# Gate tiles of the state-space part go from the inverse stage to the key stage, and all eight query tiles fill the inverse stage

## The chip, the cores and the metric

The kernel runs on one core of a Trainium2 chip. The metric is the device time of one execution in microseconds (us), the median of several runs; a shorter time is better. The core's engines work side by side, each through its own instructions in a fixed order: TensorE (PE in the profile: matrix products, with PEld its weight loads), VectorE (DVE), ScalarE (ACT), GpSimd (POOL) and SyncE (SP, which here only issues DMAs).

## What is computed

One step of a two-layer trunk over 128 context tokens and 256 latent tokens, D_MODEL = 1024, in float32. The change lies in the mixer of layer 0, which runs state-space (SSD) heads and gated DeltaNet heads from one input projection:

```python
def ssd_delta_mixer(h, ssd_h0, dn_h0, w_in, w_out, ...):
    z, xbc, dt_raw, qkv, gate, a_raw, b_raw = jnp.split(h @ w_in, _offsets(L0_SIZES), axis=-1)
    ...
    y = rmsnorm(y.reshape(bsz, length, SSD_INNER) * jax.nn.silu(z.astype(F32)), ssd_norm_w)
    qkv = jax.nn.silu(dwconv(qkv, dn_conv_w))
    q, k, v = jnp.split(qkv, [DN_QK, 2 * DN_QK], axis=-1)
    q = l2norm(q.reshape(bsz, length, DN_HEADS, DN_KEY_DIM))
    k = l2norm(k.reshape(bsz, length, DN_HEADS, DN_KEY_DIM))
    ...
    o = rmsnorm(o_f + flip(o_b), dn_norm_w) * jax.nn.silu(gate.astype(F32))...
```

`gated_delta_scan` works in chunks of 128 tokens (three here: one of context, two of latents) and needs from the keys alone, for every chunk, head and direction, the inverse of a triangular 128 x 128 matrix (`triangular_solve`). The values and queries come in only after that. So z, gate and q are products that can be computed at any time before their use.

## The kernel before

The input projection of layer 0 is cut into 56 weight tiles `w0[n]` of 128 output features: 0 to 7 keys, 8 to 15 queries, 16 to 23 values, 24 to 31 B and C of the state-space part, 32 to 39 its x, 40 to 47 its gate z, 48 to 55 the DeltaNet gate g. `proj` (L648) makes one tile: 24 matmuls (L365 to L367) with 386 columns, because each weight is split into two float32r halves. For this `fetch` (L326) loads 512 KB into one of three `wst` buffers by a DMA on SP's queue, ACT casts two halves `whi` (L335), and DVE subtracts two halves `wlo` (L338). Weights are fetched in the order of `weights` (L1707), up to three tiles ahead.

What follows a tile depends on its kind. A **convolved tile** (key, query, value, B, C, x) goes through `conv` (L658): one ACT pass (L664), four DVE taps (L670), a silu on ACT; for keys and queries then three PE transposes (L698) and three squares with a sum on ACT (L1269). A **gate tile** (z, g) takes one silu on ACT (L1291), and a DMA on ACT's queue to DRAM; DVE has only its two splits.

`delta` (L1328) runs the stages around the change, one after the other:

1. **Key stage**: `scalars` and `decay` (L779: products on DVE and POOL, L788: matmuls, L791: exp on ACT) are woven with `tile_k`, the eight key tiles (the first two are already begun in `start`). It ends with a few small DVE operations on the sums of the keys' squares, the first of them `nk` (L1348).
2. **Inverse stage**: three `inverse` generators (chunk 0 at once, chunk 2 after 8, chunk 1 after 24 units of the plan's clock: `DI`) are woven with a fill of tiles, and between two tiles of the fill goes one step of `net.quads`, modulation products (L300) whose weights `wmod` take their turn in the same three `wst` buffers. Each inverse is a long chain, mostly on DVE: N (L817), forward substitution (L857, L859), NR (L839), then pairs of small matmuls (L892, L937, L946) with work of DVE (L910, L914, L932) and ACT between them.
3. **Apply stage**: first the eight value tiles, then `apply` (L980 to L1076), woven with a fill of tiles and of `fill_qk` (the q k products, L961).

`weave` (L218) orders the work when the program is built: it keeps a clock of planned costs (4.2 for a convolved tile, 3.9 for a gate tile), advances a chain when its planned wait is over, and issues the next piece of the fill in between. A fill that is used up leaves nothing to put between the chain's steps; a fill that is left over is issued at the end of the stage (`drain`). `mix(a, b, 1)` takes one piece of a and one of b in turn. What is shown as order below is the order that results on each engine.

Of the kernel before, what the change touches and what calls it, by code (L numbers as in the profile page):

```python
# [603 lines left out]
DS = [0, 0, 0, 0]  # L604
Q1 = 4
DG = ((1, 0),)
# [12 lines left out]
class Mix0:  # L619
# [53 lines left out]
    def convs(self, base, w, b, j, ns, rest, cost=4.2, first=()):  # L673
        old, late = None, None
        for n in ns:
            if n < len(first):
                ps = first[n]
                if late:
                    late()
            else:  # L680
                ps = self.proj(base + n, self.hh, self.hl, late)
            cv = self.conv(ps, w, j + n, b)
            late = old and rest(*old)
            old = n, cv
            yield cost
        if late:
            late()
        late = rest(*old)
        if late:
            late()  # L690
        yield cost - 3.8
# [578 lines left out]

    def fill_q(self, b, e):
        def rest(n, cv):
            self.nc.scalar.activation(out=self.qT[:, n, :], in_=cv, func=AF.Silu)
            return lambda: self.norms(self.totok(self.qT[:, n, :]), self.ssq, n)
        return self.convs(8, "dn_cw", None, 8, range(b, e), rest)

# [51 lines left out]
    def delta(self, A):  # L1328
# [4 lines left out]
        with ExitStack() as c1:  # L1333
# [5 lines left out]
            self.ssq = self.ts("ssq", [3, 8])  # L1339
            fill = self.tile_k()  # L1340
            net.help = HELP[0]
# [11 lines left out]
            for d in range(2):  # L1353
                v.tensor_mul(out=self.brk[:, d], in0=rk2, in1=self.beta[:, :, 8 * d:8 * d + 8])
            v.tensor_scalar_mul(out=self.nrb, in0=self.brk, scalar1=-1.0)
            self.qT = A("qT")
            fill = mix(chain(self.fill_silu(40, self.zd), self.fill_silu(48, self.gd), self.fill_q(0, Q1)),
                       chain(net.quads(0, range(4, 8), net.wst), net.quads(1, range(Q0), net.wst)), 1)
# [6 lines left out]
        with ExitStack() as c1:  # L1365
# [7 lines left out]
            drain(self.fill_v())  # L1373
            fill = chain(self.fill_q(Q1, 8), self.fill_qk(), self.fill_bc())
            weave([late(g, d) for g, d in zip(self.apply(S0), DA + [0] * 6)], fill, W0[2])
# [331 lines left out]
def weights(t):  # L1707
# [3 lines left out]
        for n in range(8) for k in range(0, KFF, 8)]  # L1711
    o1 = lambda n, i: (t["wo1"][n, :, 1024 * i:1024 * i + 1024], 1024)
    out1 = [o1(n, i) for i in range(2) for n in range(3)] + [o1(n, i) for n in range(3, 8) for i in range(2)]
    tok = lambda js: [(t["w1t"][j, i], 1024) for j in js for i in range(2)]
    return ([(t["w0s"], 512)] + one(t["w0"], [*range(8), *range(40, 56), *range(8, 8 + Q1), *range(16, 24), *range(8 + Q1, 16), *range(24, 40)])
            + [(t["wo0"][j, :, 1024 * i:1024 * i + 1024], 1024) for i in range(2) for j in range(8)] + ffn(0) + one(t["w1f"], range(3)) + tok([4, *range(4)]) + one(t["w1f"], range(3, 18)) + out1 + ffn(1))
# [35 lines left out]
```

## Time and profile before

| | us |
|---|---|
| median of 3 runs (1462.89 to 1468.02) | 1467.04 |
| the profiled execution | 1465.71 |
| its span, first to last instruction | 1463.9 |
| busy in the span: PE / DVE / ACT | 1375.5 / 959.9 / 795.9 |
| the stretch from the key stage's first tile to `nk` | 49.6 to 110.3 |
| from `nk` to NR of the third inverse (chunk 1) | 110.3 to 204.7 |
| from there to the last matmul of that inverse | 204.7 to 247.5 |
| value tiles | 247.5 to 285.2 |
| apply | 285.2 to 372.4 |

The profile is of one execution. Its own time is 1.8 us above its span and 1.3 us under the median. Busy times are of each engine for itself and overlap, so they say nothing of who waits for whom; that is read from the single stretches.

### The profile page before, as it was taken

What the parts mean: (1) busy time and instruction counts of PE and PEld (TensorE: products, weight loads), DVE (VectorE), ACT (ScalarE), POOL (GpSimd) and SP (SyncE); (2) the same over time, 40 slices, a digit from 0 to 9 for tenths busy, and PEclk for the clock granted to TensorE, in tenths of its full rate; (3) what the DMA queues carried; (4) which work ended last, traced back from release to release, by engine and by line L of the source; (5) the groups of instructions that cost most, each with busy time, mean ns of one, the idle gap of its engine ahead of it and who ended that gap; (6) DMA issues with size and microseconds to landing.
All of it is one profiled execution on the core that took longest, in us unless ns stands there. A gap on an engine that the chain in (4) does not pass through costs nothing.

```text
span 1463.9 us, 26132 instructions
## 1 busy us (share of the span) xinstructions
PE 1375.5 (94%) x10103; PEld 1292.9 (88%) x10103; DVE 959.9 (66%) x1880; ACT 795.9 (54%) x1775; POOL 196.0 (13%) x190
## 2 busy tenths in 40 slices
PE   4979979999998999999999999999999999999996
PEld 3759869999887789789999999898999899999996
DVE  3688977865978867576666444656658477767432
ACT  4577535677475336554455444644865475555341
POOL 0042200003254403300000012100002210000001
PEclk9999989999999999799999999999999999999998
DMA  9225545312643366445554443344234434434441
GB/s 366 83 89 151 172 141 173 111 44 79 210 159 106 118 200 219 145 135 168 167 165 140 120 123 109 125 134 157 87 97 163 144 101 131 118 128 126 119 130 57
DMA packets 59899, 201.57 MB, mean 138 GB/s; under 512 B 7072, under 2 KB 11824, under 8 KB 59776
## 3 DMA queue, kind: packets, MB, share of 16 engines
q1 hardware_dynamic: 52256, 185.38, 39.9%
q10 hardware_dynamic: 6192, 9.80, 1.9%
q0 software_dynamic: 1328, 4.73, 1.1%
q8 instruction: 79, 1.29, 0.4%
q14 instruction: 44, 0.36, 0.1%
HBM read 191.20 MB, written 8.68 MB: 137 GB/s over the span
## 4 chain that ended last, share of the span: by engine, by line
PE 76%; DVE 9%; issue 5%; ACT 5%; POOL 2%; DMA 2%; ACTq 0%; POOLq 0%; DVEq 0%
PE mm L380 18%; PE mm L365 10%; PE mm L366 10%; PE mm L367 10%; PE mm L382 9%; PE pmod L300 3%; DVE wlo L338 1%; POOL er L779 1%; ACT hh L454 1%; ACT t L454 1%; PE ps L479 1%; PE ps L1575 1%; PE mmt L1500 1%; DMA wst<-w 1%; PE mmt L1501 1%
## 5 line engine op out<-in xcount | busy, mean ns | idle before, releaser
L338 DVE TENSOR_TENSOR wlo<-wst,whi 128x512 fp32r<-128x512 f32 (+1 forms) x497 | 345.8, 701 | 213.3 <-ACT whi L335 209.4
L335 ACT CAST whi<-wst 128x512 fp32r<-128x512 f32 (+1 forms) x505 | 305.0, 614 | 311.2 <-PE mm L366 166.8
L380 PE MATMUL mm<-hh,whi 128*128 128x386 f32 x728 | 247.7, 340 | 3.0 <-DVE t L571 2.8
L382 PE MATMUL mm<-hl,whi 128*128 128x386 f32 x728 | 239.2, 339 | 7.5 <-DVE hl L456 7.3
L380 PE MATMUL mm<-hh,wlo 128*128 128x386 f32 x728 | 245.3, 337 | 0.0
L365 PE MATMUL mm<-hh,whi 128*128 128x386 f32 x552 | 195.5, 354 | 6.0 <-DVE t L670 6.0
L367 PE MATMUL mm<-hh,wlo 128*128 128x386 f32 x552 | 188.9, 343 | 1.7 <-DVE wlo L338 1.7
L366 PE MATMUL mm<-hl,whi 128*128 128x386 f32 x552 | 189.8, 344 | 0.0
L382 PEld LDWEIGHTS mm<-hl,whi 128*128 128x128 f32 x728 | 135.6, 188 | 11.1 <-DVE hl L456 11.0
L380 PEld LDWEIGHTS mm<-hh,whi 128*128 128x128 f32 x728 | 137.0, 188 | 6.7 <-ACT whi L335 3.1
L380 PEld LDWEIGHTS mm<-hh,wlo 128*128 128x128 f32 x728 | 136.9, 188 | 0.6 <-DVE wlo L338 0.3
L365 PE MATMUL mm<-gh,whi 128*128 128x386 f32 x352 | 119.5, 339 | 0.0
L366 PE MATMUL mm<-gl,whi 128*128 128x386 f32 x352 | 119.2, 339 | 0.0
L367 PE MATMUL mm<-gh,wlo 128*128 128x386 f32 x352 | 118.9, 338 | 0.0
L365 PEld LDWEIGHTS mm<-hh,whi 128*128 128x128 f32 x552 | 105.7, 191 | 12.5 <-issue 11.4
L569 DVE SCALAR_TENSOR_TENSOR t<-mm,vecs,t 128x385 f32<-128x385 f32 x88 | 54.3, 619 | 88.2 <-ACT t L568 88.2
L367 PEld LDWEIGHTS mm<-hh,wlo 128*128 128x128 f32 x552 | 105.2, 191 | 2.2 <-DVE wlo L338 2.1
L366 PEld LDWEIGHTS mm<-hl,whi 128*128 128x128 f32 x552 | 105.9, 192 | 0.2
L670 DVE SCALAR_TENSOR_TENSOR t<-mm,vecs,t 128x385 f32<-128x385 f32 (+1 forms) x152 | 92.1, 614 | 11.9 <-ACT t L664 6.4
L568 ACT ACTIVATE t<-mm,vecs 128x386 f32<-128x386 f32 x88 | 59.1, 676 | 70.4 <-PE mm L382 70.4
L500 POOL TENSOR_TENSOR sums<-sums,t 128x386 f32<-128x386 f32 x36 | 41.5, 1173 | 334.8 <-PE mm L366 218.1
L300 PE MATMUL pmod<-wmod,cond 128*32 128x128 f32 x1536 | 70.6, 296 | 12.9 <-ACT t L416 12.3
(421 smaller groups left out, 2586.9 us busy)
## 6 DMA issues: line engine op xcount, KB each, us to landing
wmod<-modw_l SPq DMA_DIRECT2D x96, 512.0 KB, 4.6
wst<-up_l SPq DMA_DIRECT2D x88, 512.0 KB, 3.5
wst<-w SPq DMA_DIRECT2D x56, 512.0 KB, 3.9
wst<-wo SPq DMA_DIRECT2D x32, 512.0 KB, 3.9
wst<-down_l SPq DMA_DIRECT2D x32, 512.0 KB, 3.5
wst<-w1f SPq DMA_DIRECT2D x18, 512.0 KB, 3.6
wst<-down_l SPq DMA_DIRECT2D x16, 384.0 KB, 3.1
wst<-w1t SPq DMA_DIRECT2D x10, 512.0 KB, 3.9
```

What stands on the lines that cost most here:

```text
L300: nc.tensor.matmul(acc[32 * c:32 * c + 32, 0:128], self.cond[:, k, :], w[:, o:o + 128], start=(k == 0), stop=(k == 7), tile_position=(0, 3 ...
L335: self.conv_hi = nc.scalar.copy(out=hi[:, 0:m], in_=st[:, o:o + m])
L338: self.conv_lo = eng.tensor_sub(out=lo[:, 0:m], in0=st[:, o:o + m], in1=hi[:, 0:m].bitcast(F32))
L365: mm(ps, wh, xh, start=start, stop=False)
L366: mm(ps, wh, xl, start=False, stop=False)
L367: return mm(ps, wl, xh, start=False, stop=stop)
L380: mm(ps, w[k // 4][p][:, s], hh[:, k, :], start=(k == 0 and p == 0), stop=False)
L382: mm(ps, w[k // 4][0][:, s], hl[:, k, :], start=False, stop=(k == 7))
L500: (nc.gpsimd if i else v).tensor_add(out=acc[:, i, :], in0=acc[:, i, :], in1=p)
L568: nc.scalar.activation(out=cv, in_=ps, func=AF.Identity, scale=cw(1), bias=self.v(f"ffb_l{l}", n))
L569: stt(out=cv[:, 1:T], in0=ps[:, 0:T - 1], scalar=cw(0), in1=cv[:, 1:T], op0=ALU.mult, op1=ALU.add)
L670: nc.vector.scalar_tensor_tensor(out=o, in0=p, scalar=cw(i), in1=o, op0=ALU.mult, op1=ALU.add)
```

## The change

The eight z tiles move from the fill of the inverse stage into the key stage, one behind each key tile (`mix(self.tile_k(), self.fill_silu(40, self.zd), 1)`). The fill of the inverse stage is then the eight g tiles and all eight query tiles (before: eight z, eight g, four queries), and that of the apply stage loses the other four query tiles. The list in `weights` follows, and `convs` gives the two tiles that `start` has computed a planned cost of 0. No operation is added or taken away but loads of ACT's function tables (`ACT_TABLE_LOAD`), since exp and silu now take turns more often: from the key stage up to the first g or z tile of the inverse stage 15 stand on ACT where there were 7.

```diff
--- before.py
+++ after.py
@@ -602,7 +602,7 @@
 DI = [0, 24, 8]
 DA = [0, 0, 0]
 DS = [0, 0, 0, 0]
-Q1 = 4
+NF = 2
 DG = ((1, 0),)
 MB = [8, 4]
 W1 = 0.15
@@ -682,7 +682,7 @@
             cv = self.conv(ps, w, j + n, b)
             late = old and rest(*old)
             old = n, cv
-            yield cost
+            yield cost if n >= len(first) else 0.0
         if late:
             late()
         late = rest(*old)
@@ -1268,11 +1268,11 @@
             sq = self.n.t386()[:, 0:128]
             self.nc.scalar.activation(out=sq, in_=tr[:, c], func=AF.Square, accum_out=ss[:, c, n:n + 1])
 
-    def fill_q(self, b, e):
+    def fill_q(self):
         def rest(n, cv):
             self.nc.scalar.activation(out=self.qT[:, n, :], in_=cv, func=AF.Silu)
             return lambda: self.norms(self.totok(self.qT[:, n, :]), self.ssq, n)
-        return self.convs(8, "dn_cw", None, 8, range(b, e), rest)
+        return self.convs(8, "dn_cw", None, 8, range(8), rest)
 
     def fill_qk(self):
         self.qeps = qeps = self.ts("qeps", [3, 8])
@@ -1337,7 +1337,7 @@
             self.kT = kT = A("kT")
             self.ssk = ssk = self.ts("ssk", [3, 8])
             self.ssq = self.ts("ssq", [3, 8])
-            fill = self.tile_k()
+            fill = mix(self.tile_k(), self.fill_silu(40, self.zd), 1)
             net.help = HELP[0]
             weave([chain(self.scalars(self.pt), *(self.decay(E[c], c, 16, 8) for c in range(3)))], fill, W0[0])
             drain(fill)
@@ -1354,7 +1354,7 @@
                 v.tensor_mul(out=self.brk[:, d], in0=rk2, in1=self.beta[:, :, 8 * d:8 * d + 8])
             v.tensor_scalar_mul(out=self.nrb, in0=self.brk, scalar1=-1.0)
             self.qT = A("qT")
-            fill = mix(chain(self.fill_silu(40, self.zd), self.fill_silu(48, self.gd), self.fill_q(0, Q1)),
+            fill = mix(chain(self.fill_silu(48, self.gd), self.fill_q()),
                        chain(net.quads(0, range(4, 8), net.wst), net.quads(1, range(Q0), net.wst)), 1)
             net.help = HELP[1]
             weave([late(self.inverse(c, kT, E[c]), DI[c]) for c in range(3)], fill, W0[1])
@@ -1371,7 +1371,7 @@
                 nc.sync.dma_start(out=S0[d].rearrange("p h q -> p (h q)"), in_=t["s0dn"][:, 1024 * d:1024 * d + 1024])
             net.help = HELP[2]
             drain(self.fill_v())
-            fill = chain(self.fill_q(Q1, 8), self.fill_qk(), self.fill_bc())
+            fill = chain(self.fill_qk(), self.fill_bc())
             weave([late(g, d) for g, d in zip(self.apply(S0), DA + [0] * 6)], fill, W0[2])
             drain(fill)
 
@@ -1712,7 +1712,7 @@
     o1 = lambda n, i: (t["wo1"][n, :, 1024 * i:1024 * i + 1024], 1024)
     out1 = [o1(n, i) for i in range(2) for n in range(3)] + [o1(n, i) for n in range(3, 8) for i in range(2)]
     tok = lambda js: [(t["w1t"][j, i], 1024) for j in js for i in range(2)]
-    return ([(t["w0s"], 512)] + one(t["w0"], [*range(8), *range(40, 56), *range(8, 8 + Q1), *range(16, 24), *range(8 + Q1, 16), *range(24, 40)])
+    return ([(t["w0s"], 512)] + one(t["w0"], [*range(NF), *(j for n in range(8) for j in (n, 40 + n) if j >= NF), *range(48, 56), *range(8, 40)])
             + [(t["wo0"][j, :, 1024 * i:1024 * i + 1024], 1024) for i in range(2) for j in range(8)] + ffn(0) + one(t["w1f"], range(3)) + tok([4, *range(4)]) + one(t["w1f"], range(3, 18)) + out1 + ffn(1))
 
 
```

**PE at the end of the key stage.** A tile is 24 rows of L365 to L367; here `mm_909` is the last key tile and `mm_1070` the first z tile of before, `mm_1262` the last z tile and `mm_1374` the first g tile of now; `er` and `tri` are the decay's operands, L698 are transposes of keys, and L808 is the first matmul of an inverse. Before:

```order
L367 MATMUL mm_909<-hh_144,wlo_788 128x386
L788 MATMUL ps_892<-er_836,tri_560 128x512
L788 MATMUL ps_892<-er_838,tri_560 128x512
L365 MATMUL mm_1070<-hh_144,whi_842 128x386
L366 MATMUL mm_1070<-hl_145,whi_842 128x386
L367 MATMUL mm_1070<-hh_144,wlo_844 128x386
L365 MATMUL mm_1070<-hh_144,whi_842 128x386
L366 MATMUL mm_1070<-hl_145,whi_842 128x386
```

Now:

```order
L367 MATMUL mm_1262<-hh_144,wlo_1156 128x386
L788 MATMUL ps_1290<-er_1189,tri_608 128x512
L788 MATMUL ps_1290<-er_1191,tri_608 128x512
L698 MATMUL ps_1293<-cst_76,kT_513 128x128 x3
L788 MATMUL ps_1290<-er_1248,tri_608 128x512
L788 MATMUL ps_1290<-er_1250,tri_608 128x512
L698 MATMUL ps_1304<-cst_76,kT_513 128x128 x3
L808 MATMUL ps_1332<-kT_513 128x128 x4
L365 MATMUL mm_1374<-hh_144,whi_1195 128x386
L366 MATMUL mm_1374<-hl_145,whi_1195 128x386
L367 MATMUL mm_1374<-hh_144,wlo_1197 128x386
L808 MATMUL ps_1348<-kT_513 128x128 x4
```

The fill that stood behind the last keys' transposes now stands among the key tiles, and the first inverse begins right behind the last transposes.

**DVE ahead of NR of the third inverse** (the last row of each piece; `NR`, `TX`, `SX` and `er` belong to the inverses, `wlo` to weight tiles, `t386` with `mm` to a convolution). Before:

```order
L910 SCALAR_TENSOR_TENSOR PF_1403<-ps_2161,cst_76,PF_1403 32x8x16
L910 SCALAR_TENSOR_TENSOR PB_1404<-ps_2161,cst_76,PB_1404 32x8x16
L932 STREAM_TRANSPOSE L_2609<-PF_1403 32x8x32 x2
L932 STREAM_TRANSPOSE L_2609<-PB_1404 32x8x32 x2
L338 TENSOR_TENSOR wlo_2297<-wst_2293,whi_2295 128x512
L338 TENSOR_TENSOR wlo_2301<-wst_2293,whi_2299 128x512
L865 STREAM_TRANSPOSE TX_2261<-SX_1778 128x512
L838 TENSOR_SCALAR NR_1774<-TX_2261,cst_76 128x128
L871 TENSOR_SCALAR L_2267<-TX_2261,cst_76 128x8x16
L839 SCALAR_TENSOR_TENSOR NR_1774<-TXT_2262,cst_76,NR_1774 128x128
```

Now:

```order
L670 SCALAR_TENSOR_TENSOR t386_2602<-mm_2567,vecs_77,t386_2602 128x384
L859 TENSOR_REDUCE SX_2085<-er_2089 128x14
L670 SCALAR_TENSOR_TENSOR t386_2602<-mm_2567,vecs_77,t386_2602 128x385
L857 TENSOR_TENSOR er_2089<-SX_2085 128x225
L670 SCALAR_TENSOR_TENSOR t386_2602<-mm_2567,vecs_77,t386_2602 128x385
L859 TENSOR_REDUCE SX_2085<-er_2089 128x15
L670 SCALAR_TENSOR_TENSOR t386_2602<-mm_2567,vecs_77,t386_2602 128x384
L865 STREAM_TRANSPOSE TX_2628<-SX_2085 128x512
L865 STREAM_TRANSPOSE TXT_2629<-SX_2085 128x512
L838 TENSOR_SCALAR NR_2081<-TX_2628,cst_76 128x128
L871 TENSOR_SCALAR L_2634<-TX_2628,cst_76 128x8x16
L839 SCALAR_TENSOR_TENSOR NR_2081<-TXT_2629,cst_76,NR_2081 128x128
```

Between `nk` and this NR there now stand 24 taps L670 (six query tiles) where there were none, and 27 splits L338 for 26; eight L910, six L932 and one L872 of other inverses, ahead of it before, now come behind it.

**PE behind that NR.** `mm_2442` is the last g tile of before, `mm_2561` the first query tile; `mm_2823` is the last query tile of now and `mm_3206` the first value tile; L892 here are steps of the third and the second inverse. Before:

```order
L367 MATMUL mm_2442<-hh_144,wlo_2212 128x386
L892 MATMUL ps_2472<-Ms_2470,L_2267 32x16 x32
L892 MATMUL ps_2507<-Ms_2505,L2_2278 32x32 x32
L300 MATMUL pmod_2540<-wmod_2541,cond_83 32x128 x8
L365 MATMUL mm_2561<-hh_144,whi_2295 128x386
L366 MATMUL mm_2561<-hl_145,whi_2295 128x386
L367 MATMUL mm_2561<-hh_144,wlo_2297 128x386
```

Now:

```order
L367 MATMUL mm_2823<-hh_144,wlo_2565 128x386
L892 MATMUL ps_2867<-Ms_2865,L_2634 32x16 x32
L892 MATMUL ps_2902<-Ms_2900,L2_2645 32x32 x32
L300 MATMUL pmod_2935<-wmod_2936,cond_83 32x128 x8
L698 MATMUL ps_2946<-cst_76,qT_1329 128x128 x3
L300 MATMUL pmod_2935<-wmod_2980,cond_83 32x128 x8
L365 MATMUL mm_3206<-hh_144,whi_2662 128x386
L366 MATMUL mm_3206<-hl_145,whi_2662 128x386
L367 MATMUL mm_3206<-hh_144,wlo_2664 128x386
L365 MATMUL mm_3206<-hh_144,whi_2662 128x386
L366 MATMUL mm_3206<-hl_145,whi_2662 128x386
```

From here to the last L946 of the third inverse PE had five and three quarter tiles between the inverses' steps (g7, q0 to q3, and 18 matmuls of the first value tile); now it has two (q7 and the first value tile, cut into pieces). Of the 25 tiles that the rest of the three stages held from here on, 17 are left. In the apply stage three tiles are placed between the chains' pieces up to the last of them, where seven were; four are left for the drain, before five.

## Rows read from the trace of the kernel before

**Rows 1.** The page: span, and busy time of PE and DVE (share).

```profile
span 1463.9 us, 26132 instructions
PE 1375.5 (94%) x10103; PEld 1292.9 (88%) x10103; DVE 959.9 (66%) x1880; ACT 795.9 (54%) x1775; POOL 196.0 (13%) x190
```

**Rows 2.** Busy time by stretch: length; PE, PEld, DVE, ACT, POOL; PE clock, DMA.

```profile
49.60:110.30 60.70, 49.46 (x273) 43.12 (x271) 51.15 (x98) 40.31 (x106) 15.88 (x12) 0.94 0.29 96
...
85.65:98.40 12.75, 12.74 (x65) 11.85 (x66) 10.11 (x18) 9.66 (x36) 1.91 (x1) 0.86 0.24 82
...
110.30:204.70 94.40, 83.27 (x1030) 76.46 (x1028) 84.10 (x225) 58.27 (x132) 21.28 (x23) 0.97 0.52 160
...
204.70:212.30 7.60, 5.22 (x139) 5.05 (x140) 4.08 (x10) 0.87 (x3) 0.69 (x1) 0.52 0.46 160
212.30:247.50 35.20, 34.87 (x592) 31.62 (x590) 24.59 (x48) 19.72 (x58) 0.95 (x1) 1.00 0.52 167
...
285.20:372.40 87.20, 86.02 (x663) 84.76 (x662) 55.44 (x129) 65.92 (x236) 16.12 (x14) 1.00 0.21 67
```

**Rows 3.** PE in time, key stage: start, us, instruction, [idle before it, releaser].

```profile
66.72 0.44 PE L367 MATMUL mm<-hh,wlo 128*128 128x386 f32 x1 [1.75 <-DVE wlo L338]
...
75.30 0.50 PE L788 MATMUL ps<-er,tri 128*128 128x512 f32 x1 [1.30 <-POOL er L779]
...
78.91 0.73 PE L788 MATMUL ps<-er,tri 128*128 128x512 f32 x2 [1.05 <-DVE er L779]
85.65 0.66 PE L365 MATMUL mm<-hh,whi 128*128 128x386 f32 x1 [6.01 <-DVE t L670]
```

**Rows 4.** PE in time, around NR of the third inverse.

```profile
201.74 1.97 PE L946 MATMUL ps<-Ms,L 64*64 64x64 f32 x32 [5.91 <-ACT Ms L940]
...
208.91 0.31 PE L892 MATMUL ps<-PF,NT 32*32 32x32 f32 x2 [2.23 <-issue]
```

**Rows 5.** The chain of waits in time, 180 to 215: start, us, what.

```profile
194.55 4.49 DMA wst<-w
199.12 0.63 ACT whi L335
...
201.06 0.97 DVE TX L865
```

**Rows 6.** DVE in the stretch from `nk` to NR, by form: count, busy us, mean ns.

```profile
L338 DVE TENSOR_TENSOR wlo<-wst,whi 128x512 fp32r<-128x512 f32 x26 | 17.7, 690 | 3.2 <-ACT whi L335 3.1
...
L932 DVE STREAM_TRANSPOSE L<-PF 32x256 f32<-32x256 f32 x7 | 3.0, 431 | 0.2
...
L910 DVE SCALAR_TENSOR_TENSOR PF<-ps,cst,PF 32x128 f32<-32x128 f32 x8 | 2.8, 346 | 0.2
...
L872 DVE TENSOR_SCALAR L<-TXT,cst 128x128 f32<-128x128 f32 x3 | 2.0, 676 | 0.0
```

**Rows 7.** Busy time of the taps L670 alone, by stretch: length, DVE busy (count).

```profile
49.60:110.30 60.70, 18.42 (x32) 0.94 0.29 96
...
204.70:247.50 42.80, 9.88 (x16) 0.91 0.51 166
```

**Rows 8.** PE in time, transposes inside five value tiles on end, first and last.

```profile
256.00 0.49 PE L698 MATMUL ps<-cst,t 128*128 128x128 f32 x3
...
274.28 0.49 PE L698 MATMUL ps<-cst,t 128*128 128x128 f32 x3
```

**Rows 9.** ACT from 49 to 400 us, by form: count, busy us, mean ns.

```profile
L335 ACT CAST whi<-wst 128x512 fp32r<-128x512 f32 x98 | 59.3, 622 | 51.8 <-PE mm L366 28.1 <-DMA wst<-w 17.9 <-DVE L L914 2.4
...
L1269 ACT ACTIVATE t<-ps 128x128 f32<-128x128 f32 x48 | 12.8, 287 | 3.6 <-PE ps L698 3.4
L1269 ACT ACTIVATION_READ_ACCUMULATOR t<-ps 128x1 f32 x48 | 10.4, 217 | 0.0
L1291 ACT ACTIVATE t<-mm 128x386 f32<-128x386 f32 x16 | 7.9, 492 | 0.1
```

**Rows 10.** ACT in time: a table load and what follows it.

```profile
101.80 1.28 ACT L1262 ACT_TABLE_LOAD   x1
103.09 0.53 ACT L1262 ACTIVATE kT<-t 128x386 f32<-128x386 f32 x1
```

## The prediction

> **What bounds the kernel now.** I read the page's busy line first, because it says which engine can be the bound at all. PE is busy 94% of the span [rows 1], so over the whole program only work taken off PE, or waits and half-speed time of PE, can change the end. The change takes no work off PE. It therefore acts through PE's lost time, and I looked for that stretch by stretch [rows 2].
>
> Key stage, 60.7 us: PE is busy 49.5 and DVE 51.2. PE loses 11.2 us; four waits are 10.1 of it (1.75, 1.30, 1.05 and 6.01), and the long one ends with a DVE tap, which has to read a convolved tile's PSUM before PE may fill it again [rows 3]. After it the granted clock is 0.86 for 12.75 us [rows 2]: full speed is 2.4 GHz, the lower level 1.2, and the lost time is (1 - 0.86) x 12.75 = 1.8 us.
>
> From `nk` to NR of the third inverse, which I call the window, 94.4 us: PE 83.3 busy (0.88), DVE 84.1 (0.89). Neither is full, and each waits for the other in turn. PE loses 11.1 us. Its longest wait, 5.91 us at 195.8 to 201.7, ends with an ACT copy [rows 4]. The chain of waits runs there from a weight load (4.49 us) over ACT's `whi` to DVE's TX ahead of NR [rows 5]. So a chain on DVE sets when the third inverse may begin.
>
> Behind NR, 42.8 us to the last matmul of that inverse: PE waits 2.23 us [rows 4], and for the first 7.6 us the clock is 0.52, so PE's 5.2 busy us could have been 2.7. That is 2.5 lost by the clock and 7.6 + 35.2 - 5.2 - 34.9 = 2.7 by waiting [rows 2], about 5 us. In apply PE is busy 86.0 of 87.2 [rows 2]. It is full.
>
> What DVE does in the window is seen by form [rows 6]: a split is 0.69 us, L910 0.35, L932 0.43, L872 0.68. A tap is 18.42/32 = 0.58 us in the key stage and 9.88/16 = 0.62 behind NR [rows 7]; I take 0.6.
>
> **The change part by part.** PE's work in the three stages stays the same, so I sum the changes of lost time. A convolved tile with its three transposes takes PE (274.28 - 256.00)/4 = 4.57 us in the value tiles, of which the transposes are 0.49 [rows 8]. A gate tile, without them, is then 4.08.
>
> *Key stage.* Of eight z tiles 1.3 were already there ahead of `nk` (329 matmuls in the window of before are 13.7 tiles: 6.7 z, 7 g). So 6.7 x 4.08 = 27.3 us of PE work come in, and PE's own work is 49.5 - 1.8 + 27.3 = 75.0. DVE gets two splits a tile and no taps: 51.2 + 13 x 0.69 = 60.2. ACT has 40.3, and gets 13 casts at 0.62, 6.7 silus at 0.49 [rows 9] and eight table loads at 1.28 [rows 10]: 40.3 + 8.1 + 3.3 + 10.3 = 62.0. Both stay well below PE's 75, which was not so for DVE before (51.2 against 49.5). A z tile between two key tiles gives DVE 4.08 us of PE work for 1.4 us of splits, in which it catches up with its taps. So I let the 6.01 us wait and the half clock after it go, and keep the waits for `wlo` and `er`, 1.75 + 1.30 + 1.05 = 4.1, and 1.4 for the last transposes and squares, behind which no tile now stands ahead of `nk`: 5.5 lost for 11.2 + 1.8. That is **-7.5 us** (bounds: -12 with only the last step left, 0 if every wait stays), and `nk` comes at 49.6 + 80.5 = 130. The gate's output DMAs, one a tile on ACT's queue, move with their tiles. The weight loads, two of 256 KB a tile on SP's queue, keep their rate per tile; 14 tiles (six key, eight z) in 80.5 us for 7.3 in 60.7 would use the DMA engines about 0.29 x (14/80.5)/(7.3/60.7) = 0.42, below the 0.52 that the window shows [rows 2]. I cost them at nothing. Their cover is the three tiles of lead; without it one tile costs the 4.49 us of [rows 5].
>
> The table loads lie on ACT, in 20 us of ACT's slack. The activation behind the load at 101.80 starts 0.01 us after its end (101.80 + 1.28 = 103.08; it starts at 103.09) [rows 10]: the trace shows the price as 1.28. The Trainium skill ("ScalarE: Activation LUTs", What ACT_TABLE_LOAD costs) puts a drain of some 1.38 us beside a load of about that length, 2.66 together; it also advises gathering work by function table (Table sets: the hidden batching unit), which speaks against this change. By its price the eight new loads would be 21 us instead of 10, and the row shows no gap of such a kind.
>
> *Window.* On DVE come 24 taps of six query tiles (14.4) and one split (0.7); eight L910 (2.8), six L932 (2.6) and one L872 (0.7) now come behind NR. DVE is then 84.1 + 15.1 - 6.1 = 93.1. PE gets 15 tiles for 13.7 (5.3) and five sets of transposes (2.5), and loses the matmuls of the inverse steps that went behind NR, some 3 us by the number of those DVE steps: 88. How full DVE can be here no row says. With DVE at its present share the window is 93.1/0.891 = 104.5, with PE at its share 88/0.882 = 100, with DVE's idle time kept at 10.3 us 103.4. The two ends are 93 (DVE without a gap) and 110 (each new tap also delays a step of an inverse). I take 102, between the shares, since the chain must still go round DVE, ACT and PE for every step. PE loses 14 for 11.1: **+2.9 us** (-6 to +11). NR comes at 232 instead of 204.7.
>
> *Behind NR.* DVE's work up to the last L932 of the third inverse is about 0.7 (L872) + 16 x 0.35 + 24 x 0.43 + 4 x 0.69 + 8 x 0.6 = 24 us. PE's is two tiles (8.7), and the inverse's own 12 plus the 3 that came from ahead of NR: 24. Before, 5.75 tiles (25 us) stood between the steps. With so little cover PE must wait; how long the chain is when nothing stands in between no row shows. The ends are 24 us (no wait, -5) and 42.8 as before (19 lost, +14). I take 31: 5 of wait and 2.5 at half clock as now, 7.5 for 5, **+2.5 us**. I stay near the low end because the steps themselves are short, 0.3 to 0.7 us, and because the two other inverses' steps also fill in.
>
> *Apply.* Four query tiles (18.3 us) are gone, and three tiles stand between the chains' pieces instead of seven. ACT, 65.9 of 87.2, loses per tile two casts, two passes of some 0.5 and three squares of 0.29 + 0.22 [rows 9], 3.8 in all: 51 of 69. DVE falls from 55.4 to about 40. Neither gets fuller, so the pieces should follow as closely as now but for a place or two. **+2 us** (0 to +18, when the missing cover is lost in full).
>
> The sum is -7.5 + 2.9 + 2.5 + 2 = -0.1 us: the profiled execution's 1465.7 stays. That execution lies 1.3 us below the median, so I predict 1467.
>
> **The rivals.** *A, faster:* DVE's queue closes up. For it speaks that 0.89 of the window is busy already and that taps need no answer of a chain; against it, that all of DVE's gaps there come from the inverses' round trips, which the change does not shorten. Then the window is 97 instead of 102 (-5), the key stage keeps 2.5 of its losses instead of 5.5 (-3), and behind NR and in apply nothing is lost anew (-4.5): 1467 - 12.5 = about 1455. The Trainium skill ("Perfetto Trace Analysis", Identifying the Most-Contended Engine) goes by the engine of the highest share in a stretch. By that rule alone the window would be 93 us; the trace of before, where that engine is idle for 10.3 us, does not bear it out.
>
> *B, slower:* the third inverse runs bare. Its chain behind NR takes about 39 us instead of 31, PE waits 13 and goes at 1.2 GHz in between: +8, 1475. For it speaks that this is what the last 7.6 us ahead of 212.3 looked like, where little stood between the steps (0.52); against it, that those were 7.6 of 42.8. It decides when PE waits over 12 us there.
>
> *C, slower:* apply is short of tiles. PE waits 10 us there instead of 2, +8, 1475. Against it: ACT's and DVE's shares fall, and four tiles are still left at the end. For it: nothing is left over on PE now (1.2 of 87.2), so any new gap counts in full. It decides when PE's waits there pass 9 us.
>
> *D, slower:* each table load costs twice its row. 15 x 1.28 = 19 more on ACT make 81 in the key stage, which at the share of 0.9 of a busiest engine takes 90 us instead of 80.5: 1476. Row 103.09 speaks against it.
>
> **How the numbers follow.** Forecast 0.42, A 0.33, B 0.13, C 0.10, D 0.02. The measurement of this kernel can tell some 0.5%, 7.3 us: A gives faster, the forecast same, B, C and D slower. The range leaves out the outer part of A and of B and C (bounds of the tail and of apply at once), about 1 in 10 on each side: 1454 to 1479. The forecast alone is 1460 to 1474.
>
> **What would show it.** Right: `nk` near 130 with PE's waits ahead of it at 4 to 6 us and no 6 us wait for a tap; 15 table loads of 1.28 with no gap behind; the window near 102 with DVE at about 0.9; PE's waits behind NR near 5 and in apply at 3 at most. Wrong: a window under 97 or over 109; PE waiting over 10 us behind NR or in apply; a key stage in which ACT or DVE stays as busy as PE.

## The result, and the profile after

The changed kernel took 1452.13 us in the median of five runs (1449.12 to 1458.99), the kernel before 1468.02 beside it: a ratio of 0.9898 (95% interval 0.9874 to 0.9922). Measured once more (below) the ratio was 0.9928 (0.9913 to 0.9943). So it is faster by 0.7 to 1.0%, 10 to 15 us. The prediction, 1467 with a range of 1454 to 1479, had it as no change; the time lies on rival A's side, 2 us under the range. The median measured once more, 1456.31, lies inside the range, but the kernel before took 1467.72 beside it, so the gain stands in both.

The page's busy line of the changed kernel, to be read beside [rows 1]. Its profiled execution took 1458.99 us, the slowest of the five, so the gain in this profile (a span of 1457.2 for 1463.9) is smaller than in the medians.

```profile
span 1457.2 us, 26128 instructions
PE 1381.3 (95%) x10103; PEld 1297.3 (89%) x10103; DVE 957.2 (66%) x1880; ACT 806.5 (55%) x1785; POOL 193.4 (13%) x190
```

Busy time by stretch in the changed kernel, columns as in [rows 2]: key stage, window from `nk` to NR of the third inverse, from there to that inverse's last matmul, value tiles, and apply to about its end.

```profile
50.60:132.40 81.80, 79.26 (x434) 74.45 (x432) 61.55 (x111) 59.82 (x134) 14.03 (x12) 0.96 0.40 123
132.40:231.80 99.40, 89.32 (x1077) 82.23 (x1075) 90.22 (x233) 63.46 (x164) 20.63 (x22) 0.98 0.49 155
231.80:257.70 25.90, 23.91 (x630) 19.79 (x630) 24.47 (x58) 16.57 (x50) 1.70 (x2) 0.93 0.43 135
257.70:295.40 37.70, 37.70 (x223) 37.29 (x223) 29.71 (x52) 24.49 (x56) 0.00 (x0) 1.00 0.48 154
295.40:369.40 74.00, 71.64 (x567) 68.55 (x566) 42.65 (x107) 55.44 (x197) 19.39 (x17) 1.00 0.19 57
```

PE's loss by waiting in the key stage is 81.8 - 79.3 = 2.5 us where it was 11.2. In the window it is 10.1 where it was 11.1, behind NR 2.0 where it was 2.7. What PE waits for in the key stage now (us in all, times, longest):

```profile
PE ps L788 <- POOL er L779: 1.1, 3, 0.4
PE ps L788 <- DVE er L779: 0.5, 1, 0.5
PE ps L698 <- ACT kT L1262: 0.4, 1, 0.4
PE mm L367 <- DVE wlo L338: 0.4, 1, 0.4
```

The wait of 6.01 us for a tap [rows 3] is gone, and with it the three of over 1 us; no wait there is longer than 0.5. In the window the 5.91 us wait for ACT's `Ms` [rows 4] is gone too, but a modulation product's copy on ACT now holds PE up for 4.1 us, so that the sum is about the same:

```profile
PE pmod L306 <- ACT t L304: 5.4, 2, 4.1
PE ps L822 <- DVE N L817: 2.0, 1, 2.0
PE ps L892 <- DVE NR L839: 0.7, 1, 0.7
```

To see where the whole gain lies I cut the program, in every kernel, at three points: the first matmul of apply, the first L788 matmul of the state-space stage that follows (between the key stage's start and it stand 47 weight tiles in each of the kernels compared), and the first L365 matmul on `oh`, which belongs to the last tile of the mixer's output projection (the `oh` products of its other seven tiles are woven into the state-space stage). At the second and the third point the same work has been done in all of them; at the first it has not, as the queries and the z tiles lie on different sides of it. Of the kernel before, and then of the changed one, from the key stage's start:

```profile
49.60:285.20 235.60, 210.52 (x2251) 193.49 (x2249) 192.72 (x426) 143.76 (x354) 38.80 (x35) 0.96 0.44 138
285.20:393.39 108.19, 107.01 (x782) 105.75 (x781) 75.66 (x161) 75.66 (x252) 20.22 (x18) 1.00 0.31 98
393.39:545.60 152.21, 139.11 (x1015) 113.44 (x1014) 119.57 (x210) 75.39 (x163) 55.78 (x46) 0.97 0.46 147
```

```profile
50.60:295.40 244.80, 230.19 (x2359) 213.75 (x2357) 205.94 (x451) 164.34 (x402) 36.36 (x35) 0.97 0.45 142
295.40:388.30 92.90, 90.54 (x674) 87.45 (x673) 61.04 (x139) 65.22 (x214) 20.97 (x18) 1.00 0.30 95
388.30:537.60 149.30, 138.27 (x1014) 112.54 (x1014) 118.46 (x206) 77.25 (x163) 54.76 (x46) 0.97 0.45 148
```

The three stages that the change touches went from 235.6 + 108.2 = 343.8 to 337.7 us, 6.1 less. The stage behind them, which I call the next stage and in which the diff changes nothing, took 149.3 instead of 152.2. The kernel before was profiled once, so its 343.8 and 152.2 are of one execution.

### The profile page after: what moved, and what is told of

Read it like the earlier page. It is cut to its first block, busy times and chain, and to the rows that moved or that the text cites. A ratio compares the mean times of both kernels' runs of the same rounds, so it can differ in the third digit from the quotient of the medians.

```text
span 1457.2 us, 26128 instructions
## 1 busy us (share of the span) xinstructions
PE 1381.3 (95%) x10103; PEld 1297.3 (89%) x10103; DVE 957.2 (66%) x1880; ACT 806.5 (55%) x1785; POOL 193.4 (13%) x190
## 4 chain that ended last, share of the span: by engine, by line
PE 79%; DVE 12%; issue 4%; POOL 3%; ACT 2%; DMA 0%; POOLq 0%; DVEq 0%; ACTq 0%
PE mm L380 18%; PE mm L365 11%; PE mm L366 11%; PE mm L367 11%; PE mm L382 9%; PE pmod L300 3%; DVE t L670 2%; DVE wlo L338 1%; POOL xres L535 1%; PE ps L479 1%; PE ps L1575 1%; PE mmt L1500 1%; DVE er L779 1%; PE mmt L1501 1%; PE mmt L1502 1%
## 5 line engine op out<-in xcount | busy, mean ns | idle before, releaser
L338 DVE TENSOR_TENSOR wlo<-wst,whi 128x512 fp32r<-128x512 f32 (+1 forms) x497 | 345.6, 701 | 201.0 <-ACT whi L335 196.5
L365 PE MATMUL mm<-hh,whi 128*128 128x386 f32 x552 | 195.5, 354 | 0.0
L367 PE MATMUL mm<-hh,wlo 128*128 128x386 f32 x552 | 189.8, 344 | 0.4 <-DVE wlo L338 0.4
L365 PE MATMUL mm<-gh,whi 128*128 128x386 f32 x352 | 119.5, 339 | 0.0
L367 PE MATMUL mm<-gh,wlo 128*128 128x386 f32 x352 | 118.9, 338 | 0.0
L365 PEld LDWEIGHTS mm<-hh,whi 128*128 128x128 f32 x552 | 105.7, 191 | 6.1 <-issue 4.8
L367 PEld LDWEIGHTS mm<-hh,wlo 128*128 128x128 f32 x552 | 105.5, 191 | 1.1 <-DVE wlo L338 0.7
L670 DVE SCALAR_TENSOR_TENSOR t<-mm,vecs,t 128x384 f32<-128x384 f32 (+1 forms) x152 | 92.7, 613 | 10.8 <-ACT t L664 7.3
L300 PE MATMUL pmod<-wmod,cond 128*32 128x128 f32 x1536 | 70.9, 297 | 12.8 <-ACT t L416 12.5
```

What stands on the lines that cost most here:

```text
L300: nc.tensor.matmul(acc[32 * c:32 * c + 32, 0:128], self.cond[:, k, :], w[:, o:o + 128], start=(k == 0), stop=(k == 7), tile_position=(0, 3 ...
L338: self.conv_lo = eng.tensor_sub(out=lo[:, 0:m], in0=st[:, o:o + m], in1=hi[:, 0:m].bitcast(F32))
L365: mm(ps, wh, xh, start=start, stop=False)
L367: return mm(ps, wl, xh, start=False, stop=stop)
L670: nc.vector.scalar_tensor_tensor(out=o, in0=p, scalar=cw(i), in1=o, op0=ALU.mult, op1=ALU.add)
```

## The experiments

Each was compared with the kernel before on the same chip; the ratios are to that kernel. Of each edit the lines that move or add work are shown; the list in `weights` follows them, and `fill_q` and `fill_bc` take a range of tiles where one is named. The first theory was that the gain is PE's lost time in the key stage, which the gate tiles fill, with the later stages as good as before.

**The changed kernel once more** (no edit).

> The changed kernel once more, for a second profile and a second ratio. Theory 1 (the waits of PE that the gate tiles fill in the key stage are the gain, the later stages stay as they were): key stage 82 us with 2.5 us of PE waits, the three stages 9 to 10 us shorter than before, and the median 9 to 15 us under the kernel before, as the profiled execution of after lay on the slow side of its five. Theory 2 (the profiled stages show the whole gain, and the rest of the 15 us was scatter): a median only 7 to 9 us under the kernel before.

1456.31 us, ratio 0.9928, 11.4 us under the kernel before. The three stages took 337.4 us, as in the first profile; the next one was shorter than there:

```profile
387.47:533.20 145.73, 135.90 (x1014) 111.47 (x1014) 115.76 (x205) 76.97 (x163) 56.37 (x46) 0.98 0.48 152
```

So the changed kernel repeats its three stages, 6 us under the one profile of the kernel before, and the next stage adds 3 to 6. Theory 1 had the median right but not the place: it wanted the three stages 9 to 10 us shorter, and needed a further place. Theory 2, with 7 to 9 us in all, had too little.

**The z tiles alone**, with four query tiles left in apply:

```diff
-            fill = mix(chain(self.fill_silu(48, self.gd), self.fill_q()),
+            fill = mix(chain(self.fill_silu(48, self.gd), self.fill_q(0, 4)),
...
-            fill = chain(self.fill_qk(), self.fill_bc())
+            fill = chain(self.fill_q(4, 8), self.fill_qk(), self.fill_bc())
```

> The z tiles go to the key stage, but four query tiles stay in apply, so the inverse stage has 12 tiles to fill it where the changed kernel has 16. Theory 1 (the gain is the key stage): key stage 82 us as in the changed kernel. The window from nk to NR is then set by DVE: 90.2 less 12 to 16 taps and 6 splits, 77 to 80 us busy, at most 90 us long, with PE waiting 8 us or more than now, and behind NR PE has only modulation products: it waits 8 to 12 us there. Sum 1460 to 1468. Rival (the chains of the inverses are long by themselves, and only the cover hides it): the window stays at 97 to 99 and the tail at 25 or more, PE waits 20 us more, 1470 to 1478. Rival (filling the inverse stage with queries gives nothing): 1452, as the changed kernel.

1462.17 us, ratio 0.996 (0.9939 to 0.9981). The window, and behind NR:

```profile
131.70:227.60 95.90, 84.37 (x1026) 75.26 (x1026) 85.52 (x226) 55.98 (x144) 20.50 (x22) 0.91 0.51 160
227.60:247.40 19.80, 18.02 (x587) 14.74 (x585) 17.33 (x43) 13.69 (x31) 1.73 (x2) 0.91 0.24 72
```

Two things are to be seen. With four tiles fewer (18.3 us of PE work) the way from `nk` to apply is 282.8 - 131.7 = 151.1 us where the changed kernel has 163.0, so 6.4 of the 18.3 us come back. They come back mostly at half speed: window and tail (from NR to the inverse's last matmul) lose 0.09 x 115.7 = 10.4 us to the clock instead of some 4, and PE waits 13.3 us there for 12.1. This is the part of theory 1 that held: the hole that the z tiles fill in the key stage opens again, in part, in the inverse stage unless queries fill it. Its sizes did not hold: the window, 95.9, is nearer the rival's 97 to 99 than theory 1's 90 at most, and PE waits 1.8 us behind NR, not 8 to 12. And behind NR the third inverse takes 19.8 us with little but modulation products and pieces of one tile between its steps. The chain there by itself is no longer than that; no row had shown it ahead, and for the tail the rival that it is long by itself is refuted.

**The queries alone**, with z left in the inverse stage (24 tiles there) and the old planned cost of 4.2 for the two tiles of `start`:

```diff
-            fill = mix(self.tile_k(), self.fill_silu(40, self.zd), 1)
+            fill = self.tile_k()
...
-            fill = mix(chain(self.fill_silu(48, self.gd), self.fill_q()),
+            fill = mix(chain(self.fill_silu(40, self.zd), self.fill_silu(48, self.gd), self.fill_q()),
```

> The eight z tiles stay in the inverse stage, and all eight queries go there too (24 tiles), so the key stage is that of before. Theory 1 (the gain is the key stage): key stage 60.7 us with PE's 6 us wait for a tap, window and tail as before, no gain: 1464 to 1470. Rival (the gain comes from the queries leaving apply, and from what then stands around the inverses): 1455 to 1460.

1465.42 us, ratio 0.9985 (0.9974 to 0.9996): next to nothing. In the key stage PE waits again for a tap, in total, times, longest:

```profile
PE mm L365 <- DVE t L670: 4.1, 1, 4.1
PE ps L788 <- DVE er L779: 2.1, 1, 2.1
```

By the three cuts, the same stretches as above:

```profile
49.20:305.40 256.20, 233.50 (x2359) 215.72 (x2357) 208.94 (x451) 155.06 (x394) 37.05 (x35) 0.94 0.44 136
305.40:397.98 92.58, 90.49 (x675) 87.51 (x673) 61.19 (x139) 65.18 (x214) 20.94 (x18) 1.00 0.31 95
397.98:546.00 148.02, 136.60 (x1015) 111.00 (x1014) 118.56 (x206) 77.28 (x163) 54.82 (x46) 0.98 0.46 150
```

The three stages are 348.8 us, 5 longer than before, with (1 - 0.94) x 256 = 15 us lost to the clock where the kernel before lost 9; the next stage is 4 shorter. In the three stages z alone gives 2.6 us (341.2 for 343.8), the queries alone cost 5, and both together give 6: there each needs the other. In the next stage the time of these kernels goes with the queries: 152.2 and 154.3 without their move, 148.0, 149.3 and 145.7 with it. Of the whole time the parts alone give 0.4% and 0.15%, together 0.7 to 1.0%.

**Other tiles in the key stage**: B and C, with their taps, in place of z.

```diff
-            fill = mix(self.tile_k(), self.fill_silu(40, self.zd), 1)
+            fill = mix(self.tile_k(), self.fill_bc(), 1)
...
-            fill = chain(self.fill_qk(), self.fill_bc())
+            fill = chain(self.fill_qk(), self.fill_silu(40, self.zd))
```

> As the changed kernel, but the eight B and C tiles, each with four taps on DVE, stand between the key tiles, and the z tiles are made where B and C were, behind the apply stage's chains. Same number of tiles of the same planned cost. Theory 1a (gate tiles fill the key stage because they cost DVE little): DVE gets 61.6 + 32 x 0.58 = 80 us of work against PE's 79, the waits for taps come back, key stage 88 to 92, the whole 1458 to 1463. Rival 1b (any tile fills it; PE only lacked work): key stage 82 to 84, the whole 1450 to 1455.

1469.84 us, ratio 1.0015. Its key stage:

```profile
49.80:131.60 81.80, 77.51 (x438) 73.60 (x436) 74.60 (x143) 61.87 (x138) 14.81 (x12) 0.98 0.39 121
```

It is as long as with gate tiles, 81.8 us, although DVE has 74.6 us of work instead of 61.6. In the key stage rival 1b holds: PE lacked work, and B and C tiles fill it as well as z tiles; that gate tiles spare DVE, as I had argued, is not what counts. The expected total was wrong all the same: from apply's start to the second cut it took 97.4 us for 92.9, and the next stage 158.1 for 149.3. What stands there decided the time, and that is the place that theory 1 lacked.

**B and C tiles in place of the queries** in the inverse stage (z in the key stage, four queries still in apply):

```diff
-            fill = mix(chain(self.fill_silu(48, self.gd), self.fill_q()),
+            fill = mix(chain(self.fill_silu(48, self.gd), self.fill_q(0, 4), self.fill_bc(0, 4)),
...
-            fill = chain(self.fill_qk(), self.fill_bc())
+            fill = chain(self.fill_q(4, 8), self.fill_qk(), self.fill_bc(4, 8))
```

> The z tiles in the key stage; in the inverse stage eight g, four query and four B or C tiles; the other four queries stay in apply, and four B and C tiles fewer are left behind it. Theory 1 (the inverse stage needs its 16 tiles, whichever, taken from stages in which PE is full): as the changed kernel within 4 us, 1450 to 1457, the queries in apply cost nothing. Rival (it matters that the queries leave apply, or that their squares are done early): 1460 to 1464, as when the z tiles alone were moved.

1462.08 us, ratio 0.9956. The three cuts:

```profile
50.40:294.20 243.80, 228.52 (x2347) 212.48 (x2345) 205.11 (x450) 161.78 (x378) 36.34 (x35) 0.97 0.47 146
294.20:386.29 92.09, 90.24 (x686) 88.76 (x685) 60.39 (x135) 67.77 (x239) 20.18 (x18) 1.00 0.24 75
386.29:543.40 157.11, 141.91 (x1014) 115.56 (x1014) 125.08 (x211) 74.06 (x161) 53.38 (x46) 0.95 0.46 148
```

The three stages take 335.9 us, no more than in the changed kernel: there it doesn't matter whether queries or B and C fill the inverse stage. But the total is the rival's, since the next stage takes 157.1. Its waits of PE for `xd`, a product on DVE (L1189), in this kernel, then in the kernel before, then in the changed one:

```profile
PE ps L1193 <- DVE xd L1189: 4.3, 1, 4.3
```

```profile
PE ps L1193 <- DVE xd L1189: 3.2, 1, 3.2
```

```profile
PE ps L1193 <- DVE xd L1189: 0.6, 2, 0.3
```

By this wait the 14 profiles fall into two groups. In nine (the changed kernel twice, queries alone, and six kernels below: `q_first`, `cost_42` and the four with more work) it is 0.6 us at most in all, and the stage takes 143.8 to 149.3 us. In five it is one wait of over 2 us, and the stage takes 151.4 to 158.1: before (3.2), z alone (3.2), B and C for queries (4.3), and also B and C in the key stage and `denser14` below, in which all queries are in the inverse stage:

```profile
PE ps L1193 <- DVE xd L1189: 5.1, 1, 5.1
PE ps L1193 <- DVE xd L1189: 2.7, 1, 2.7
```

So the place of the queries alone does not decide it. What goes with the wait is the order of the instructions. On PE the kernel with z alone has in this stage row by row the order of the kernel before, on DVE too but for one row; the one with queries alone has on both the order of the changed kernel; the other three of the five have orders of their own. The order that the build makes behind apply differs with what stood ahead. Between the two first profiles, 152.2 and 149.3, the wait is 2.6 of the 2.9 us, at a granted clock of 0.97 in both. The further 3.5 us of the repeat came at the same order, with a clock of 0.98; they are scatter between executions.

**More work on DVE**: three products of 128 x 386 for each g tile, unused.

```diff
             z = net.t386()
+            for _ in range(3 if base == 48 else 0):
+                nc.vector.tensor_tensor(out=self.junk, in0=net.cst[:, 0:386], in1=net.cst[:, 0:386], op=ALU.mult)
```

> The changed kernel with three products of 128 x 386 on DVE added to each g tile (24 in the inverse stage, of some 0.5 us, 12 us in all; their result is not used). Theory 1 (DVE has no room in the window: its share of 0.91 is all it can reach): the window grows from 99.4 to (90.2 + 12)/0.91 = 112, the median by 10 to 13. Rival (DVE's idle 9 us take up work that no chain waits for): the window grows by less than 6 us.

The products, which read a constant only, all ran in the first 48.9 us of the program, so this says nothing on the window; 1450.97 us, ratio 0.9901, is the changed kernel a third time (three stages 335.6, next 147.3). Then with products that read the tile's silu:

```diff
+            for _ in range(3 if base == 48 else 0):
+                nc.vector.tensor_tensor(out=self.junk, in0=z, in1=z, op=ALU.mult)
             nc.scalar.dma_start(out=out[n], in_=z)
```

> As dve_more, but the three products of each g tile read that tile's silu, so they cannot run ahead of the inverse stage (24 of some 0.5 us, 12 us of DVE work between nk and NR; their result is not used). Theory 1 (DVE's queue and the inverses' round trips set the window; DVE can't get past a share of about 0.91): window 106 to 112 instead of 99.3, median 7 to 13 us above the changed kernel. Rival (neither engine is full, and work that no chain waits for goes into the gaps of DVE as 8 us of matmuls went into those of PE): window up to 103, median within 4 us of the changed kernel.

**More work on PE**: the first three matmuls of each g tile twice.

```diff
+        if n >= 48:
+            net.acc(ps, w, 0, hh[:, 0, :], hl[:, 0, :], True, True)
         for k in range(8):
```

> The changed kernel with the first three matmuls of each g tile done twice (24 more of 0.34 us, 8.2 us of PE; the second time starts the sum anew, so the output stays). Theory 1 (the window is as long as DVE's queue and the inverses' round trips make it; PE's 10 us of waits are room): the window grows by 0 to 3 us, the median by under 4. Rival (PE's own work sets the window at its share of 0.90): it grows by 8 to 9, and the median too.

The window with the late products, and with the matmuls:

```profile
131.30:235.90 104.60, 97.03 (x1101) 88.02 (x1099) 99.07 (x257) 67.10 (x170) 22.91 (x22) 0.97 0.46 147
```

```profile
130.40:229.70 99.30, 92.29 (x1081) 86.02 (x1081) 90.65 (x232) 63.96 (x159) 22.34 (x21) 0.97 0.48 155
```

9 us more of DVE's busy time lengthened the window by 5 (DVE's share rose to 0.95), between what the two theories had expected; the total, 1456.58 us (0.992), hardly shows it, since the next stage came out at 143.8. The matmuls left the window at 99.3 us; up to the inverse's last matmul it was 126.6 instead of 125.3, and the total 1455.27 (0.9918). But they were a smaller load than I had expected. A record of 0.34 us is not what a matmul adds: the 24 of a tile take 4.08 us, so 24 more are some 4 us, not 8.2. From `nk` to apply, in the changed kernel, with the late products, and with the matmuls:

```profile
132.40:295.40 163.00, 150.93 (x1928) 139.31 (x1927) 144.40 (x340) 104.52 (x269) 22.33 (x23) 0.98 0.48 151
131.30:299.70 168.40, 156.90 (x1934) 142.88 (x1933) 152.91 (x365) 105.02 (x269) 24.60 (x23) 0.96 0.47 147
130.40:294.90 164.50, 153.86 (x1953) 143.52 (x1952) 145.03 (x340) 105.26 (x269) 24.32 (x23) 0.97 0.47 150
```

8.5 us more on DVE lengthened this by 5.4, and 2.9 us more on PE by 1.5. Each engine took up part of its load in its gaps; which of the two is nearer to a bound these two runs don't show.

**More changes of ACT's table** in the key stage:

```diff
+                if base == 40:
+                    nc.scalar.activation(out=self.junk, in_=net.eps, func=AF.Exp)
                 nc.scalar.activation(out=z, in_=ps, func=AF.Silu)
```

> The changed kernel with a 128 x 1 exp ahead of the silu of each z tile, so that ACT changes its function table 25 times in the key stage instead of 15 (10 more loads, 12.8 us, and 8 small exps). By the row (1.28 us a load and nothing behind it) ACT has 59.8 + 13 + 2 = 75 us of work in 82: key stage 82 to 84, median 0 to 3 us longer than the changed kernel. Rival (each change of table costs twice the row, as the drain that the Trainium skill tells of in ScalarE: Activation LUTs, What ACT_TABLE_LOAD costs): ACT 59.8 + 25 x 1.38 + 15 = over 100 us, key stage 100 or more, median 18 or more above the changed kernel.

1454.22 us, ratio 0.9911. ACT in time there:

```profile
89.70 1.28 ACT L1292 ACT_TABLE_LOAD   x1
91.00 0.20 ACT L1292 ACTIVATE junk<-eps 128x1 f32<-128x1 f32 x1
91.22 1.28 ACT L1293 ACT_TABLE_LOAD   x1
92.51 0.49 ACT L1293 ACTIVATE t<-mm 128x386 f32<-128x386 f32 x1
```

Each activation starts 0.01 or 0.02 us after its load has ended, and ACT was busy 75.0 us as worked out from the row. The key stage was 85.9 us, 2 to 4 more than expected, but PE had 42 matmuls more in it, which then weren't needed in the window: up to apply the kernel took 246.3 us for 244.8. The Trainium skill ("ScalarE: Activation LUTs", What ACT_TABLE_LOAD costs) puts a drain of some 1.38 us beside the load; it does not show here.

**The queries ahead of the g tiles** in the inverse stage:

```diff
-            fill = mix(chain(self.fill_silu(48, self.gd), self.fill_q()),
+            fill = mix(chain(self.fill_q(), self.fill_silu(48, self.gd)),
```

> The changed kernel with the eight query tiles ahead of the eight g tiles in the inverse stage. The taps then lie beside the forward substitutions and the first two inverses, and DVE has only splits beside the third. Theory 1 (DVE's total work sets the window and the tail together): window and tail together 125 us as in the changed kernel, median within 3 us of it. Rival (taps in the tail delay the third inverse's steps): the tail is 3 to 6 us shorter and the median too.

1453.69 us, ratio 0.9903. Window and tail were 91.3 + 30.8 = 122.1 us for 125.3, up to apply 243.5 for 244.8. The tail was longer, not shorter; 16 more matmuls of tiles stood behind NR. No difference that counts.

**Two tiles more** in the inverse stage, and longer planned waits:

```diff
-W0 = [1, 1.2, 1, 1]
+W0 = [1, 1.4, 1, 1]
...
-            fill = mix(chain(self.fill_silu(48, self.gd), self.fill_q()),
+            fill = mix(chain(self.fill_silu(48, self.gd), self.fill_q(), self.fill_bc(0, 2)),
```

> The changed kernel with two B and C tiles more in the inverse stage (18 instead of 16), and the planned waits of the inverses' chains 1.4 instead of 1.2 times, so that one tile more stands ahead of the third NR. Theory 1 (PE has about 10 us of waits left in the inverse stage that more tiles fill): window and tail together 125 to 131, 8 to 9 us of later PE work gone, the whole 3 to 8 us under the changed kernel. Rival (the two tiles' taps and splits lengthen DVE's queue by 7 us, and the window with it): the same time as the changed kernel, or up to 4 us longer.

1460.56 us, ratio 0.9956 (0.9931 to 0.998): by its median slower than the changed kernel. Up to apply it took 255.8 us, 11 more, apply gave back 9.5, and the next stage was 151.4. The three stages together took 339.2 for 337.7: the two tiles' 8 us of PE work gained nothing where they now stand, though with both edits made at once the tiles and the planned waits can't be told apart. And the order behind apply changed for the worse. No version tried beats the changed kernel.

**The old planned cost** for the two tiles of `start`:

```diff
-            yield cost if n >= len(first) else 0.0
+            yield cost
```

> The changed kernel with the old planned cost of 4.2, in place of 0, for the two key tiles that start has already computed. Theory 1 (it only shifts the decay's pieces by two places among the key tiles, PE keeps a tile between any two): key stage 82 to 84 us, median within 3 us of the changed kernel. Rival (the planned cost is what keeps PE from waiting for er): PE's waits in the key stage come back, 4 us or more, and the median is 4 us or more longer.

1456.38 us, ratio 0.9918. Key stage 83.5 us with 7 matmuls more in it, three stages 339.1, next 146.8: this part of the change is worth 0 to 2 us.

## Why the prediction was wrong

*What bounds it now* was right: PE's lost time is what changed, and PE's work did not. The forecast failed at three of its steps: the wait behind NR, the wait in the window, and the program behind apply, which the sum left out.

*Key stage* (forecast 80.5 us, measured 81.8, 81.9 and, in the profile of `dve_more`, 79.8): right in size, for a reason that was half wrong. Waits fell to 2.5, 3.9 and 3.3, further than the 5.5 that I had kept, but the half clock that I let go stayed in part: the granted clock was 0.96, 0.98 and 1.00 in these three. (Before, the row's 0.94 was 0.06 x 60.7 = 3.6 us, of which I had counted the 1.8 behind the long wait.) And it is not the gate tiles' light load on DVE that did it.

*Window* (forecast 102, measured 99.4 and 99.1): DVE was busy 90.2 instead of 93.1, at the share of 0.91 that I had reckoned with, and PE lost 10.1 us, not 14. The term +2.9 measured -1.0 by waits: PE's busy time rose by 6 us, and its waits did not grow with it.

*Behind NR* (forecast 31, measured 25.9 twice): this is the step whose length failed most. PE's work there was nearly right, 24 us forecast and 23.9 busy, of which some 1.8 is half clock. But I let PE wait 5 us for want of cover, between no wait and the tail's length before, 42.8 us, although PE was busy 40.1 of that. It was long because it was full of tiles. With the pieces of one in between the chain takes at most 19.8, and PE's wait with two tiles is 2.0 and 1.8, not 5; the half clock cost 0.07 x 25.9 = 1.8, not 2.5. The term +2.5 measured -1.4. Rival B rested on the same misreading and fell with it.

*Apply* (forecast +2): the cut from apply's start on went from 108.2 to 92.9, which is 15.3 less for 18.3 us of tiles: +3. Right in kind, and rival C's 8 us did not come.

In lengths these are +1.3 in the key stage, -2.6 in the window, -5.1 behind NR and +1 from apply on: -5.4 together, most of the difference between the forecast -0.1 and the -6 to -8 us of the three stages. The rest is a place that my sum left out: I let the program behind apply stay as it was, without a reason. It gained 3 to 6 us there, as the two groups of kernels show. That the order differs behind apply, and that PE then waits 2.6 us less for `xd`, is shown; which rule of the build moved it, and whether more of the stage's difference than that wait is due to the order, stays open.

*Rival A* was the nearest: it had a window of 97, 2.5 us lost in the key stage and no new loss behind. Its reason, that DVE's queue closes up, is not borne out: DVE's share in the window rose from 0.89 to 0.91 only, and more DVE work still found room. That its total of 1455 came so near is in part luck: it took 12.5 us off in the three stages, which gave 6 to 8, and the next stage, which it did not name, gave the others. *Rival D* is refuted by the experiment with more tables.

## What to carry to other kernels

A hole in one stage is worth filling only with work from a stage in which PE is full; taken from a stage that hides latency with it, the hole moves in part, so two moves that are worth little alone can be worth something together. The length of a chain is not read from a stretch in which the cover itself keeps PE busy: take out the cover, or count its work first. When a build orders instructions by itself, compare the order of the next stages too, since they can change without a line of theirs in the diff.

## What was not expected of the hardware

Two kernels with the same order of work on PE at this place (the changed one, and `dve_more`) lose different time to the clock in the same 20 us at the end of the mixer's output projection. The stretches below begin at the same matmul in both; first the changed kernel, then `dve_more`:

```profile
571.80:575.60 3.80, 2.83 (x17) 2.52 (x15) 3.80 (x5) 2.46 (x6) 3.47 (x3) 1.00 0.75 252
575.60:587.60 12.00, 10.19 (x76) 8.40 (x77) 4.75 (x9) 4.53 (x11) 3.31 (x5) 0.66 0.31 97
587.60:591.60 4.00, 4.00 (x24) 3.32 (x24) 0.00 (x0) 0.78 (x3) 0.01 (x1) 0.50 0.61 241
```

```profile
566.30:570.10 3.80, 2.79 (x16) 2.47 (x14) 3.80 (x6) 2.25 (x6) 3.48 (x3) 1.00 0.67 225
570.10:582.10 12.00, 10.45 (x83) 8.84 (x84) 4.49 (x8) 4.86 (x13) 3.05 (x5) 0.72 0.30 86
582.10:586.10 4.00, 3.61 (x50) 2.73 (x48) 1.73 (x8) 0.66 (x3) 1.00 (x2) 1.00 0.89 321
```

Where the first row ends and the second begins PE waits for DVE; these are the rows that end the wait, of 2.61 us in the changed kernel and of 2.38 in `dve_more`:

```profile
577.24 0.61 PE L479 MATMUL ps<-cst,sums 128*128 128x1 f32 x4 [2.61 <-DVE sums L500]
571.48 0.27 PE L479 MATMUL ps<-cst,sums 128*128 128x1 f32 x1 [2.38 <-DVE sums L500]
```

Then PE goes at 1.2 GHz, in `dve_more` for (1 - 0.72) x 12 / 0.5 = some 7 us, in the changed kernel to the end of its rows and on to 596.6, 17 us in all, with 24 matmuls in the last 4 us of the rows for 50. The length of the wait does not settle it: in `q_first` PE waits 2.61 us there too, and the clock is down for some 7 us. Why it stays down longer in one execution than in another stays open. The executions of one kernel, here 1449 to 1459, differ by some us, and this is one place where some of it arises; stretches cut at equal work tell more than a single total.
